# Moving four pieces of a hybrid attention layer: two matmul groups a slot later, a reduction behind a solve, and a new last block

## The chip, the cores and the metric

The kernel runs on one core of a Trainium2 chip. A core has a matrix engine (TensorE, PE in the profile, with its weight loads listed as PEld), a vector engine (VectorE, DVE), a scalar engine (ScalarE, ACT), a general engine (GpSimd, POOL), and SyncE (SP), which here issues almost all DMA transfers. Each engine works through its own queue in order. Engines wait for one another through semaphores. TensorE writes to PSUM; the other data lie in SBUF, and DRAM is reached by DMA. The metric is the device time of one execution in microseconds (us).

## The reference

The layer takes a residual stream of 256 positions by 4096 columns. One projection feeds 16 heads of forgetting attention ("fox", width 128), 32 heads of an RWKV-7 recurrence (width 64) and a gate. The gated heads go through an output projection, and a post-LayerNorm closes the layer. Cut to what matters here:

```python
proj = jnp.einsum('bsd,dc->bsc', x, w_in)
# rwkv columns: shift by one position, then split
w_raw = -jax.nn.softplus(-(w0 + jnp.tanh(wd) @ w_up)) - 0.5     # LoRA product
decay = jnp.exp(-jnp.exp(w_raw))
a = jax.nn.sigmoid(a0 + ad @ a_up)                              # LoRA product
# one step of the recurrence
sa = jnp.einsum('bhvk,bhk->bhv', state, a_t)
state = (state * w_t[:, :, None, :] + sa[..., None] * b_t[:, :, None, :]
         + v_t[..., None] * k_t[:, :, None, :])
y_t = jnp.einsum('bhvk,bhk->bhv', state, r_t)
# readout: GroupNorm of y per head, a bonus term, then
h = jnp.concatenate([fox_out, rwkv_out], axis=-1) * jax.nn.silu(z)
out = jnp.einsum('bsc,cd->bsd', h, w_out)
x = _layernorm(ALPHA * x + out, ln_gain, ln_bias, LN_EPS)
```

## The kernel before

**The main stream.** The 256 positions are two halves of 128 (`m`). Columns of the input projection come in blocks of 512. For each of eight head pairs `n` there are four blocks `b`: r and k of two 128-column groups (b = 0), v and the fox v (b = 1), and fox q, k and both gates of one group each (b = 2, 3). A block needs 32 contraction tiles. Each fp32 weight tile of two contraction tiles is split into a high and a low part: ScalarE casts the high part (L141), VectorE subtracts to get the low part (L142). Three matmuls (L147, L148, L149) then stand for one exact product, so a block is 192 main matmuls. Weights are loaded by SP three tiles ahead.

**Slots.** All other work of the layer is written as Python generators (`ahead`, `chain`, `unload`, `fox`). After every six main matmuls, `slot()` advances each generator to its next `yield`. A `yield` thus means "traced one slot later". `wait(n)` yields n times. The instructions of a slot are put behind the latest low-part split on VectorE. A planner then fixes each engine's order: it keeps the traced order where it thinks an instruction ready in time, and may move others. Two ways to bind it are used: `tc.keep_in_program_order` puts an instruction behind the one traced before it on its engine, and `tc.issue_after(i)` puts what is traced in its block behind instruction `i` on that engine. Both bind the order of issue only.

**The recurrence.** `ahead` runs `prepare(i)` for each of the 16 column groups in turn. It starts with `front(i)`: split of the LoRA weights (`uph` on ScalarE at L420, `upl` on VectorE at L422), load of the next LoRA weights (`load_up`), a `yield`, the LoRA product `lp` (L428 to L430), two Tanh, another `yield`, the decays, another `yield`. It then waits until the r and k columns of its group are there (`rk`, made at L276). The even group of a pair starts only when the pair before is `done`.

`chain` runs `rwkv(n)` for each pair. It forms the products `gp` (L534); solves a triangular system of 32 rows by 31 steps of a product and a reduce on VectorE (L601, L604), a step per slot; sends the result through DRAM (`td`, `T`); sums the values for their mean (`vm`, L616) and writes centred values into SV by eight VectorE operations (L623); builds the inverse from the blocks (`qt`, `xp`); and then goes through four chunks. A chunk has `rh` (L647), whose result R is copied by both VectorE and ScalarE (L650); `up` (L678), whose result is copied into UV (L681) by both; and, save in the last chunk, the state update `sp` (L687), from UV to the next SV (L691, L693). The readout `yp` (L707, L709) follows, then GroupNorm and the gating with the split of h (`gate`, L378, L382), and `done`. The end of block b = 2 needs `n in turned`, which `rwkv(n)` sets after `gp`.

**The output projection and the end.** Eight output blocks `b` of 512 columns follow, each with 32 contraction tiles, three matmuls each (L880 to L882), for both halves. The slots go on through most of the first two. `add(m, b)` adds the residual and takes `bn_stats`; `gain(m, b)` multiplies by the LayerNorm gain. For half 0, `moments(0)` comes while half 1's last matmuls still run. For half 1 it comes at the very end: `add(1, 7)`, the aggregation of all eight blocks' statistics (L1001), standard deviation, its reciprocal `rs`, and `s2` = mean times `rs`. A small matrix of these factors is transposed by TensorE (`zp`, `zpa`, copied as `l1` and `la`), so that one matmul with `rows` gives the LayerNorm's remaining terms for a block. Blocks 4 to 7 of half 1 (HALVED = 4) are finished by `finish`: a matmul `wp` and one VectorE operation (L1033). Blocks 0 to 3 have been gathered in PSUM with their gain; they take one matmul with `la` (L1063) and a ScalarE multiplication (L1064). Each finished block is stored by SP (L1027) in the order in which the loop writes them.

Of the kernel before, what the change touches and what calls it, by code (L numbers as in the profile page):

```python
# [10 lines left out]
F32 = mybir.dt.float32  # L11
# [6 lines left out]
P = 128  # L18
# [66 lines left out]
def layer(ctx: ExitStack, tc: tile.TileContext, xt, xtok, w_main, w_lora, w_first, muv, w_o, up, par, mulora, fbias, lng, lnb, cst, out):  # L85
# [331 lines left out]
    def front(i):  # L417
# [5 lines left out]
        load_up(i + 1)  # L423
        yield
        lp = pst(f"lp{i}")
# [94 lines left out]
    def rwkv(n):  # L520
# [78 lines left out]
        for t, s in enumerate(range(B - 2, -1, -1)):  # L599
            w = B - 1 - s  # L600
            first = nc.vector.tensor_tensor(prod[:, :, :, s + 1 :], nb[:, :, s : s + 1, s + 1 :].to_broadcast([P, 2, NJ, w]), xc[:, :, :, s + 1 :], ALU.mult)  # L601
            if not t or not n:
                tc.keep_in_program_order(first)
            nc.vector.tensor_reduce(xc[:, :, :, s : s + 1], prod[:, :, :, s:], AX.X, ALU.add)  # L604
            next(other, None)
            if t % ROWS == ROWS - 1:
                yield
# [7 lines left out]
        vt = vs_[n].rearrange("p m (u j v) -> p m u j v", u=2, j=2)  # L615
        tc.keep_in_program_order(nc.vector.tensor_reduce(vm.rearrange("p m u j -> p (m u j)"), vs_[n].rearrange("p m (a v) -> p (m a) v", v=HD), AX.X, ALU.add))  # L616
        yield
# [53 lines left out]
        for c in range(NCH):  # L671
# [11 lines left out]
            if c == NCH - 1:  # L683
                break
            sp = pst(f"sp{n}_{c}")
            for u in range(2):
# [198 lines left out]
    late = []  # L885
    st = [const.tile([P, NB, 6], F32, name=f"lst{m}") for m in range(2)]

    def add(m, b):
        acc = oacc[b]
        o = slice(b * OB, (b + 1) * OB)  # L890
        nc.vector.scalar_tensor_tensor(res[m][:, o], res[m][:, o], ALPHA, acc[m], ALU.mult, ALU.add)
        nc.vector.bn_stats(st[m][:, b, :], res[m][:, o])

# [47 lines left out]
    for b, q in outs:  # L941
# [22 lines left out]
        if b == 0:  # L964
            while sides:
                slot()
            mid.close()
            rpool = ctx.enter_context(tc.tile_pool(name="rpool", bufs=1))
            res = [rpool.tile([P, D], F32, tag=f"res{m}", name=f"res{m}") for m in range(2)]
            rows = rpool.tile([P, D], F32R, name="rows")  # L970
            nc.gpsimd.memset(rows.bitcast(F32), 0.0)
            identr = rpool.tile([P, P], F32R, name="identr")
            nc.vector.tensor_copy(identr, ident)
            for n in range(2):
                load_tok(n)
            lneps = const.tile([P, 1], F32, name="lneps")
            nc.vector.memset(lneps, LN_EPS)
# [5 lines left out]

    rss = []

    def factors(m, name):
# [4 lines left out]
    def moments(m):  # L991
# [8 lines left out]
        add(m, NB - 1)  # L1000
        nc.vector.bn_aggr(mv, st[m].rearrange("p b s -> p (b s)"))  # L1001
        mean = mv[:, 0:1]
# [4 lines left out]
        nc.vector.tensor_copy(z[:, 0:3:2], zh.bitcast(F32).to_broadcast([P, 2]))  # L1007
        last = nc.vector.tensor_tensor(z[:, 1:2], s2, zh.bitcast(F32), ALU.subtract)
        if m:
            for n, (v, at) in enumerate(((mean, (slice(0, 3, 2), slice(1, 2))), (sd, (slice(3, 5), slice(5, 6))))):  # L1010
# [44 lines left out]
    with tc.issue_after(last):  # L1055
        l1 = row(z1, "1", pp, "pp")
        la = row(za, "a", pp, "pp")
        gain(1, NB - 1)
    for n in range(HALVED):
        b = HALVED + n  # L1060
        finish(1, b, l1, pp, "pp")
        o = slice(n * OB, (n + 1) * OB)
        nc.tensor.matmul(wps[n], la, rows[:, o], start=False, stop=True)  # L1063
        nc.scalar.mul(res[1][:, o], wps[n], rss[1])  # L1064
        store(1, b, 1)
        store(1, n, 1)
# [51 lines left out]
```

## Time and profile before

| what | us |
| --- | --- |
| median of three runs | 1921.87 (1921.42 to 1925.38) |
| profiled execution | 1921.7 |
| its span, first to last instruction | 1919.5 |
| TensorE busy | 1906.1 |
| VectorE busy | 1375.6 |
| ScalarE busy | 987.3 |
| GpSimd busy | 259.1 |

A row of the timeline gives start, duration, engine, line, operation, tiles written and read, shapes, and a count where equal neighbours are merged; in brackets stands the idle time ahead of it and what ended it. Matmuls overlap one another, so the spacing of their starts says more than their durations. A row of the table of waits gives who waited for whom, the total in us, how often, and the longest. The summary of a line lists how long its engine sat idle before it and until what.

### The profile page before, as it was taken

Reading aid. Unit: us, or ns where it says so; the run is one execution under the profiler, and the core shown is the slowest. Engines: PE = TensorE matmul, PEld = TensorE weight load, DVE = VectorE, ACT = ScalarE, POOL = GpSimd, SP = SyncE. Lnnn points to the kernel's source line nnn. Section 1 sums busy time; section 2 is a strip of 40 time slices with the busy share of each in tenths; the row PEclk is TensorE's granted clock in tenths of the full one; section 3 lists DMA queues with packets and bytes.
Section 4 is the critical chain, followed back from the end, with each engine's and each line's share of the span. In section 5 each row is a group of like instructions: output and inputs, shape, how many; then the busy total and the mean of one; then the engine's idle time right before and its main releaser. Section 6 shows DMA issues by size and latency. Waiting matters only on the chain.

```text
span 1919.5 us, 27983 instructions
## 1 busy us (share of the span) xinstructions
PE 1906.1 (99%) x9785; PEld 1583.1 (82%) x9785; DVE 1375.6 (72%) x2355; ACT 987.3 (51%) x1543; POOL 259.1 (13%) x463
## 2 busy tenths in 40 slices
PE   9999999999999999999999999999999999999998
PEld 9878788888888888888888888888888878888886
DVE  7677768776876688677867786778677856755555
ACT  6554555456545644564456454645474554434333
POOL 0022012111310131013101300140013001000000
PEclk9999999999999999999999999999999999999999
DMA  9577667867686768677766776677667876766564
GB/s 344 154 232 230 193 188 229 242 202 208 209 249 194 225 204 244 195 217 217 237 199 213 223 232 203 212 225 223 206 211 221 276 257 231 253 200 202 186 203 165
DMA packets 269393, 420.04 MB, mean 219 GB/s; under 512 B 142338, under 2 KB 169364, under 8 KB 269252
## 3 DMA queue, kind: packets, MB, share of 16 engines
q1 hardware_dynamic: 268820, 417.58, 70.2%
q8 instruction: 76, 1.25, 0.3%
q10 hardware_dynamic: 432, 0.69, 0.1%
q14 instruction: 65, 0.53, 0.1%
HBM read 388.55 MB, written 29.64 MB: 218 GB/s over the span
## 4 chain that ended last, share of the span: by engine, by line
PE 96%; DVE 2%; DMA 1%; ACT 1%; issue 0%; SPq 0%; DVEq 0%; ACTq 0%
PE acc L147 24%; PE acc L149 23%; PE acc L148 23%; PE oacc L882 6%; PE oacc L880 6%; PE oacc L881 6%; PE gp L534 1%; PE rh L647 1%; PE up L678 1%; PE sp L687 1%; PE accl L149 1%; PE accl L147 1%; DMA w<-in_w_main_dram 1%; PE accl L148 0%; PE yp L709 0%
## 5 line engine op out<-in xcount | busy, mean ns | idle before, releaser
L759 POOL COPY pT<-lg 32x96 f32<-32x96 f32 x128 | 59.6, 466 | 406.7 <-DVE lg L755 402.0
L571 POOL COPY BKt<-BK 32x192 f32<-32x192 f32 x128 | 76.8, 600 | 55.2 <-DVE BK L568 50.2
L604 DVE TENSOR_REDUCE xc<-prod 128x8 f32<-128x16 f32 (+30 forms) x248 | 72.2, 291 | 5.5
L601 DVE TENSOR_TENSOR prod<-Nb,xc 128x8 f32<-128x8 f32 (+30 forms) x248 | 72.1, 291 | 3.6
L142 DVE TENSOR_TENSOR w_6l<-w,w_6h 128x1024 fp32r<-128x1024 f32 x31 | 39.8, 1283 | 40.6 <-ACT w_6h L141 23.4
L142 DVE TENSOR_TENSOR w_14l<-w,w_14h 128x1024 fp32r<-128x1024 f32 x31 | 38.0, 1225 | 39.4 <-ACT w_14h L141 33.3
L141 ACT CAST w_13h<-w 128x1024 fp32r<-128x1024 f32 x31 | 32.6, 1052 | 45.8 <-issue 12.3
L141 ACT CAST w_12h<-w 128x1024 fp32r<-128x1024 f32 x31 | 32.6, 1051 | 45.8 <-PE acc L148 26.5
L142 DVE TENSOR_TENSOR w_8l<-w,w_8h 128x1024 fp32r<-128x1024 f32 x31 | 37.8, 1220 | 25.4 <-ACT w_8h L141 17.2
L142 DVE TENSOR_TENSOR w_13l<-w,w_13h 128x1024 fp32r<-128x1024 f32 x31 | 38.3, 1234 | 23.6 <-ACT w_13h L141 12.1
L142 DVE TENSOR_TENSOR w_7l<-w,w_7h 128x1024 fp32r<-128x1024 f32 x31 | 37.9, 1222 | 20.5 <-ACT w_7h L141 8.0
L142 DVE TENSOR_TENSOR w_12l<-w,w_12h 128x1024 fp32r<-128x1024 f32 x31 | 38.9, 1256 | 18.8 <-ACT w_12h L141 10.3
L142 DVE TENSOR_TENSOR w_5l<-w,w_5h 128x1024 fp32r<-128x1024 f32 x31 | 39.7, 1282 | 16.8 <-PE acc L149 10.5
L142 DVE TENSOR_TENSOR w_11l<-w,w_11h 128x1024 fp32r<-128x1024 f32 x31 | 38.2, 1232 | 18.0 <-issue 12.4
L141 ACT CAST w_9h<-w 128x1024 fp32r<-128x1024 f32 x31 | 32.5, 1050 | 35.9 <-PE acc L148 25.5
L142 DVE TENSOR_TENSOR w_3l<-w,w_3h 128x1024 fp32r<-128x1024 f32 x31 | 37.9, 1222 | 18.0 <-ACT w_3h L141 10.2
L147 PE MATMUL acc<-w_5h,x 128*128 128x512 f32 x124 | 50.6, 408 | 0.0
L147 PE MATMUL acc<-w_8h,x 128*128 128x512 f32 x124 | 50.5, 408 | 0.0
L149 PE MATMUL acc<-w_2l,x 128*128 128x512 f32 x124 | 48.4, 391 | 1.4 <-DVE w_2l L142 1.4
L147 PE MATMUL acc<-w_15h,x 128*128 128x512 f32 x124 | 49.6, 400 | 0.0
L147 PE MATMUL acc<-w_11h,x 128*128 128x512 f32 x124 | 49.1, 396 | 0.4 <-ACT w_11h L141 0.4
L147 PE MATMUL acc<-w_9h,x 128*128 128x512 f32 x124 | 49.5, 399 | 0.0
(812 smaller groups left out, 6605.1 us busy)
## 6 DMA issues: line engine op xcount, KB each, us to landing
w<-in_w_main_dram SPq DMA_DIRECT2D x496, 512.0 KB
wo<-in_w_o_dram SPq DMA_DIRECT2D x128, 512.0 KB
bt<-bk SPq DMA_DIRECT2D x88, 128.0 KB
Nb<-nd SPq DMA_DIRECT2D x16, 512.0 KB
hd<-hl SPq DMA_DIRECT2D x29, 256.0 KB
h<-hd SPq DMA_DIRECT2D x29, 256.0 KB
wr<-in_w_first_dram SPq DMA_DIRECT2D x15, 384.0 KB
lr<-in_w_lora_dram SPq DMA_DIRECT2D x14, 336.0 KB
```

The costliest lines, as they stand in the source:

```text
L141: nc.scalar.copy(hi[:, :n], src[:, :n])
L142: latest[0] = nc.vector.tensor_tensor(lo[:, :n], src[:, :n], hi[:, :n].bitcast(F32), ALU.subtract)
L147: nc.tensor.matmul(acc[:, :n], xs[k][:, 0, tt], hi[:, o : o + n], start=(k == 0), stop=False)
L148: nc.tensor.matmul(acc[:, :n], xs[k][:, 1, tt], hi[:, o : o + n], start=False, stop=False)
L149: nc.tensor.matmul(acc[:, :n], xs[k][:, 0, tt], lo[:, o : o + n], start=False, stop=(k == KT - 1))
L571: nc.gpsimd.tensor_copy(BKt[B * b : B * (b + 1), :, :, B * a : B * (a + 1)], BK[B * a : B * (a + 1), :, : NCH - 1, B * b : B * (b + 1)])
L601: first = nc.vector.tensor_tensor(prod[:, :, :, s + 1 :], nb[:, :, s : s + 1, s + 1 :].to_broadcast([P, 2, NJ, w]), xc[:, :, :, s + 1 :], ...
L604: nc.vector.tensor_reduce(xc[:, :, :, s : s + 1], prod[:, :, :, s:], AX.X, ALU.add)
L759: (nc.gpsimd.tensor_copy if b % 2 else nc.scalar.copy)(pT[B * b : B * (b + 1), :, B * a : B * (a + 1)], lg[B * a : B * (a + 1), :, B * b : ...
L880: nc.tensor.matmul(acc, ht[k][:, 0, tt], hi, start=(k == 0), stop=False)
L881: nc.tensor.matmul(acc, ht[k][:, 1, tt], hi, start=False, stop=False)
L882: nc.tensor.matmul(acc, ht[k][:, 0, tt], lo, start=False, stop=(k == KT - 1))
```

## The change

- `front`: the LoRA product is traced two slots after the split of its weights, not one.
- `rwkv`: one more `yield` stands ahead of the update `sp` of each chunk but the last.
- `rwkv`: the reduce that makes `vm` is queued behind the last reduce of the solve on VectorE, and no longer behind whatever was traced there just before.
- The end: for half 1, the statistics of output blocks 0 to 6 are aggregated when block 6 is done, and kept as one triple (count, mean, count times variance) beside the six numbers of block 7, so that the last aggregation reads 9 columns and not 48.
- The end: block 4 of half 1 is finished by VectorE alone. Its gain and bias are loaded early into `own`, broadcast over the partitions. Two operations then give `res * rs - (gain * s2 - bias)`, and it is stored first. `gain(1, 7)` comes later, just ahead of the finish of block 7.

```diff
@@ front
         load_up(i + 1)
-        yield
+        yield from wait(2)
         lp = pst(f"lp{i}")
@@ rwkv
-            nc.vector.tensor_reduce(xc[:, :, :, s : s + 1], prod[:, :, :, s:], AX.X, ALU.add)
+            solved = nc.vector.tensor_reduce(xc[:, :, :, s : s + 1], prod[:, :, :, s:], AX.X, ALU.add)
...
-        tc.keep_in_program_order(nc.vector.tensor_reduce(vm.rearrange("p m u j -> p (m u j)"), vs_[n].rearrange("p m (a v) -> p (m a) v", v=HD), AX.X, ALU.add))
+        with tc.issue_after(solved.ins):
+            nc.vector.tensor_reduce(vm.rearrange("p m u j -> p (m u j)"), vs_[n].rearrange("p m (a v) -> p (m a) v", v=HD), AX.X, ALU.add)
...
             if c == NCH - 1:
                 break
+            yield
             sp = pst(f"sp{n}_{c}")
@@ add
+    sums = const.tile([P, 9], F32, name="sums")
...
-        nc.vector.bn_stats(st[m][:, b, :], res[m][:, o])
+        nc.vector.bn_stats(sums[:, 3:] if m and b == NB - 1 else st[m][:, b, :], res[m][:, o])
+        if m and b == NB - 2:
+            nc.vector.bn_aggr(sums[:, 1:3], st[m][:, : NB - 1].rearrange("p b s -> p (b s)"))
+            nc.vector.memset(sums[:, 0:1], float(b * OB + OB))
+            nc.vector.tensor_scalar(sums[:, 2:3], sums[:, 2:3], float(b * OB + OB), None, ALU.mult)
@@ after output block 0
+            own = rpool.tile([P, 2, OB], F32, name="own")
+            for j, src in enumerate((lng, lnb)):
+                nc.sync.dma_start(out=own[:, j, :], in_=src[:, HALVED * OB : (HALVED + 1) * OB].to_broadcast([P, OB]))
@@ moments
-        nc.vector.bn_aggr(mv, st[m].rearrange("p b s -> p (b s)"))
+        nc.vector.bn_aggr(mv, sums if m else st[m].rearrange("p b s -> p (b s)"))
...
+        s2s.append(s2)
@@ the end, half 1
     with tc.issue_after(last):
         l1 = row(z1, "1", pp, "pp")
         la = row(za, "a", pp, "pp")
-        gain(1, NB - 1)
+        o = slice(HALVED * OB, (HALVED + 1) * OB)
+        nc.vector.scalar_tensor_tensor(own[:, 0, :], own[:, 0, :], s2s[1], own[:, 1, :], ALU.mult, ALU.subtract)
+        ahead_ = nc.vector.scalar_tensor_tensor(res[1][:, o], res[1][:, o], rss[1], own[:, 0, :], ALU.mult, ALU.subtract)
+        store(1, HALVED, 1)
     for n in range(HALVED):
         b = HALVED + n
-        finish(1, b, l1, pp, "pp")
+        with tc.issue_after(ahead_.ins):
+            if b == NB - 1:
+                gain(1, b)
+            if n:
+                finish(1, b, l1, pp, "pp")
         o = slice(n * OB, (n + 1) * OB)
         nc.tensor.matmul(wps[n], la, rows[:, o], start=False, stop=True)
         nc.scalar.mul(res[1][:, o], wps[n], rss[1])
-        store(1, b, 1)
+        if n:
+            store(1, b, 1)
         store(1, n, 1)
```

1 line of the change is left out of this document (added).

## The prediction

> **What bounds the kernel now.** I read the page first, then the table of who waited for whom on TensorE, then single places in the timeline.
>
> ```profile
> span 1919.5 us, 27983 instructions
> PE 1906.1 (99%) x9785; PEld 1583.1 (82%) x9785; DVE 1375.6 (72%) x2355; ACT 987.3 (51%) x1543; POOL 259.1 (13%) x463
> ```
>
> TensorE (PE) is busy in all but 13.4 us of the span. The change removes one matmul of 9785, so it can save time in three places only: stalls between matmuls, the end, where TensorE has run dry, and the start, which it does not touch. The table of waits names the stalls long enough to be counted one by one:
>
> ```profile
> PE acc L149 <- DVE w_2l L142: 1.4, 1, 1.4
> PE zp L1020 <- DVE zd L1008: 1.4, 1, 1.4
> ...
> PE acc L149 <- DVE w_10l L142: 1.0, 1, 1.0
> PE up L678 <- ACT R L650: 0.9, 1, 0.9
> PE acc L147 <- ACT w_11h L141: 0.4, 1, 0.4
> ```
>
> Each occurs once. Everything that this change can win is of this size: single microseconds in 1900. A change of 0.2% (3.8 us of the median of 1921.87) is about what a measurement of this kernel can tell from none.
>
> The sum below is made against the profiled execution: 1921.7 us, of which 1919.5 are span and 2.2 lie around it. The median of the runs is 0.2 us above it, so I count the two as one.
>
> **Part 1: the state update a slot later.** For three of the four chunks of a pair, the matmul `sp` (L687) is now traced one slot, six main matmuls, after `up`. It reads UV, which ScalarE and VectorE copy out of PSUM (L681). The summary of line 687, and three of its groups in the timeline, each with the main matmul before and after:
>
> ```profile
>   DVE UV L681: 3.5, 13
> ```
>
> ```profile
> 615.04 0.39 PE L149 MATMUL acc<-w_6l,x 128*128 128x512 f32 x1
> ...
> 615.64 0.48 PE L147 MATMUL acc<-w_7h,x 128*128 128x512 f32 x1
> ...
> 606.72 0.40 PE L149 MATMUL acc<-w_4l,x 128*128 128x512 f32 x1
> ...
> 607.39 0.47 PE L147 MATMUL acc<-w_4h,x 128*128 128x512 f32 x1
> ...
> 623.25 0.40 PE L149 MATMUL acc<-w_9l,x 128*128 128x512 f32 x1
> ...
> 623.98 0.48 PE L147 MATMUL acc<-w_9h,x 128*128 128x512 f32 x1
> ```
>
> From start to start the first group takes 0.60 us, the second 0.67, the third 0.73: the last two lose 0.07 and 0.13 us. The summary counts 13 such waits; its 3.5 us adds idle time of the weight-load queue to that of the array, so it is no price. Thirteen times 0.07 to 0.13 is 0.9 to 1.7 us. I take 1.4, since the larger loss is the more frequent. It should go wholly: one slot is six times the 0.23 us between main matmuls, 1.4 us, and no wait here is longer than a tenth of that. From below I allow nothing gained. The yield adds no instruction, DMA or semaphore.
>
> What becomes later is the chain behind it: the three updates move the readout of a pair and `done` by three slots, and with Part 2 by four, 5.5 us. The next to wait for that is `prepare` of the next pair, which starts with the LoRA product. In the rows below its first matmul is at 842.45 and VectorE first touches the new r and k columns at 857.63, 15.2 us later.
>
> ```profile
> 842.45 0.28 PE L428 MATMUL lp<-lr,uph 96*128 96x256 f32 x1
> ...
> 843.85 0.34 PE L430 MATMUL lp<-lr,upl 96*128 96x256 f32 x1
> 844.03 0.28 PE L428 MATMUL lp<-lr,uph 96*128 96x256 f32 x1
> ```
>
> ```profile
> 857.63 0.88 DVE L276 SCALAR_TENSOR_TENSOR s<-raw,prm,s 128x255 f32<-128x255 f32 x2
> ```
>
> Two more slots of `front` follow the product (2.8 us), so 12.4 us are spare, against 5 slots needed (6.9 us). The pair loop therefore does not grow, and I cost the delay at nothing. If that cover were gone, `chain` would slip by the missing slots in each pair, until `turned` held back the next eviction.
>
> **Part 2: the LoRA product a slot later.** L430 reads `upl`, which VectorE makes at L422. The summary of line 430 and a clean group:
>
> ```profile
>   DVE upl L422: 1.3, 6
> ```
>
> ```profile
> 871.01 0.28 PE L430 MATMUL lp<-lr,upl 96*128 96x256 f32 x1
> 871.13 0.28 PE L428 MATMUL lp<-lr,uph 96*128 96x256 f32 x1
> ```
>
> A clean L430 is followed after 0.12 us. The one at 843.85 took 0.18, so it lost 0.06. Six such waits give 0.4 us from below and the summary gives 1.3 from above (again with the load queue's idle time). I take 0.6, near the lower end, because that end is a spacing of the array itself. The extra slot lies ahead of the two Tanh on ScalarE (L432, L434) and all of `front` behind them, whose cover is the 12.4 us just counted. `load_up` keeps its place on SP.
>
> **Part 3: the sum of the values behind the solve.** The wait of 1.4 us for w_2l stands in the first pair. The VectorE rows ahead of it, and the matmul that waited:
>
> ```profile
> 208.17 0.68 DVE L616 TENSOR_REDUCE vm<-vs 128x8 f32<-128x512 f32 x1
> ...
> 209.17 0.28 DVE L623 SCALAR_TENSOR_TENSOR SV<-vm,vs 64x128 f32<-64x128 f32 x1
> ...
> 214.66 1.22 DVE L142 TENSOR_TENSOR w_2l<-w,w_2h 128x1024 fp32r<-128x1024 f32 x1
> ...
> 217.25 0.41 DVE L604 TENSOR_REDUCE xc<-prod 128x8 f32<-128x256 f32 x1
> ```
>
> ```profile
> 215.93 0.50 PE L149 MATMUL acc<-w_2l,x 128*128 128x512 f32 x1 [1.45 <-DVE w_2l L142]
> ```
>
> VectorE has no gap in this stretch. The reduce (0.68) and eight STT of 0.28 stand between the last steps of the solve and ahead of the split: 2.9 us that nothing needs before `rh`. Behind the last step of the solve, they also stand behind w_2l, which starts ahead of the last step now (its reduce is the row at 217.25). 2.9 us is more than 1.45, so I take the whole 1.4. The ends are 1.4 gained and, if the same 2.9 us then delay a later split by as much, nothing. In the later pairs the same move wins nothing, because the table has no wait there.
>
> **Part 4: the end.** The rows of the tail, from the aggregation to the stores, and the stretch in which the stores run:
>
> ```profile
> 1908.14 0.37 DVE L1001 BATCH_NORM_AGGREGATE mv<-lst 128x2 f32<-128x48 f32 x1
> ...
> 1909.08 0.16 DVE L1005 TENSOR_TENSOR s<-mv,rs 128x1 f32<-128x1 f32 x1
> ...
> 1909.67 0.68 DVE L896 TENSOR_TENSOR res<-res,lg 128x512 f32<-128x512 f32 x1
> ...
> 1910.40 0.27 ACT L1022 CAST la<-zpa 128x128 fp32r<-128x128 f32 x1
> ...
> 1911.09 2.81 DVE L1033 SCALAR_TENSOR_TENSOR res<-res,rs,wp 128x512 f32<-128x512 f32 x4 [0.74 <-PE wp L1032]
> ...
> 1911.33 2.09 ACT L1064 ACTIVATE res<-wp,rs 128x512 f32<-128x512 f32 x3 [0.65 <-PE wp L1063]
> ```
>
> ```profile
> 1911.87 0.81 SPq L1027 DMA_DIRECT2D out_dram<-res  x2
> ```
>
> ```profile
> 1913.00:1918.00 5.00, 0.54 (x2) 0.00 (x0) 0.90 (x2) 1.10 (x2) 0.00 (x0) 0.50 1.03 382
> ```
>
> The last eight stores are 2.1 MB, and at 382 GB/s with a DMA share of 1.03 they need 5.5 us, 0.69 each. The DMA engines are the bound from the first of these stores on, so the end moves with the first, as long as the next ones are there. The aggregation shrinks from 48 elements to 9: between the 0.37 of today and the 0.16 of a one-column operation I take 0.27, a gain of 0.1. Then `own` takes two STT, each priced at the 0.70 of L1033 (2.81 for four), from 1909.57: done at 1910.97, so that the first store leaves at about 1911.0 and not at 1911.87, 0.9 us sooner. The second is ScalarE's first product, ready at about 1911.9 (1911.33 less 0.1, and 2.09 / 3 = 0.70). It follows the first by 0.9 us, and the first keeps the engines for 0.69, which leaves a hole of 0.2. Gain 0.6 to 0.7, of which I take 0.6; the ends are 0 (stores bound by their data) and 0.9. VectorE's total from 1909.57 on is two STT, the gain and three finishes, 4.2 us, so its last block is ready at 1913.8, when only four stores have gone: covered. One matmul fewer shortens nothing by itself.
>
> TensorE's clock shows here too: the stretch above was granted 0.50, after the 1.4 us that the table of waits shows ahead of `zp`. [...]
>
> The other additions: two broadcast loads of 256 KB into `own` on SP after output block 0, at most 0.52 MB at 382 GB/s, 1.4 us of transfer ahead of the next weight loads. I cost them at nothing, since the table of waits has no TensorE wait for a DMA; uncovered, they cost 1.4 us. The early aggregation, memset and scale after block 6 are 0.7 us of VectorE beside projection matmuls, and nothing is queued behind them but `gain` and the splits of block 7.
>
> **The sum.** 1.4 + 0.6 + 1.4 + 0.6 = 4.0 us: 1921.7 - 4.0 = 1917.7. The waits for w_10l, R and w_11h are outside the edits; I count them as unchanged.
>
> **Rivals.** *The written slot is not the issued place.* At 842.45 and 843.85 the two matmuls L428 and L430 are written back to back and issued 1.4 us apart, with main matmuls between: the order is made by a planner with its own idea of what is ready. If it puts `sp` and L430 again right behind their producers, Parts 1 and 2 win nothing: 1921.7 - 2.0 = 1919.7. Against it: the 13 waits of line 687 come about because `sp` stands where it is written, close behind its producers.
>
> *The re-timed chain makes new single waits.* For it speak the four waits of the table, all at places where VectorE, ScalarE or the SP queue bunch up, and one of the long SP waits, from the table of the SP queue between 265 and 300 us:
>
> ```profile
> SPq L281 <- DVE tw L436: 5.4, 1, 5.4
> ```
>
> In the first two pairs the chain moves most. Four new waits like the four listed are 3.7 us, and the time would be 1921.4. Against it: the wait for w_11h follows that SP wait, and a later `front` takes the LoRA operations out of its way, so it may as well win 0.4.
>
> *Slower: the readout meets the block boundary.* The split with little lead in the steady pairs is w_2l, just after output of block 0 of a pair:
>
> ```profile
> 836.81 0.42 DVE L378 SCALAR_TENSOR_TENSOR h<-post,zr 128x256 f32<-128x256 f32 x1
> ...
> 838.73 1.22 DVE L142 TENSOR_TENSOR w_2l<-w,w_2h 128x1024 fp32r<-128x1024 f32 x1
> ```
>
> ```profile
> 841.55 0.39 PE L149 MATMUL acc<-w_2l,x 128*128 128x512 f32 x1
> ```
>
> It is ready at 839.95, 1.6 us ahead of its use. The readout of a pair is two halves of four operations like the one of 0.42, 3.4 us. If four slots' delay put all of it newly ahead of one such split, TensorE would wait 1.8 us in each of six pairs, 10.8 us: 1921.7 - 4.0 + 10.8 = 1928.5. It decides from 2.9 us of extra VectorE work ahead of the split (1.6, and 7.8 us over six pairs). Against it: half of that work stands ahead of this split already, and moving it later takes it away from there.
>
> **How the numbers follow.** Forecast 0.50, with a range of its own from 1916.0 (the waits for R and w_11h go as well) to 1919.0 (Part 3 or Part 4 falls short). Planner's order 0.13, new waits 0.21, slower 0.11, and 0.05 that more waits go than I count, below 1916. Faster by over 0.2% is below 1918.0: four fifths of the forecast and the last case, 0.45 less a little for noise, 0.44. Slower is above 1925.7: 0.11 and a little of the new waits, 0.13. Within: 0.43. The range from 1915.8 to 1922.5 holds all cases but the slower one and the far end.
>
> **What would show it.** Part 1: no idle time on line 687. Part 2: none on L430. Part 3: L616 and L623 behind the last L604 in every pair, and no wait for w_2l. Part 4: the first of the last eight stores leaves SP some 0.9 us sooner relative to the aggregation, and the end follows by 0.6. The prediction is wrong if the table of TensorE's waits has new rows over 1 us, or if pairs come further apart than they do now.

## The result and the profile after

The changed kernel takes 1917.48 us (median of 14 runs, 1916.41 to 1920.35), the kernel before 1922.75 (median of 14, 1921.42 to 1925.61): a ratio of 0.9975, with a 95% interval from 0.9968 to 0.9982. That is a gain of some 5 us, where 1917.7 was predicted. The profiled execution of the changed kernel took 1917.13 us, with a span of 1915.3, 4.2 us below that of before.

Line numbers behind the edits move by two or more: the update `sp` is L689 now, its result UV is copied at L682, `vm` is at L617 and SV at L624. First the head of the page, which has the busy time, its share of the span and the instructions of each engine:

```profile
span 1915.3 us, 27998 instructions
PE 1903.0 (99%) x9784; PEld 1584.8 (83%) x9784; DVE 1398.3 (73%) x2359; ACT 985.9 (51%) x1543; POOL 261.5 (14%) x463
```

TensorE idles for 12.3 us of the span now, against 13.4. So most of the gain is not idle time in the sense of this line: its busy time fell by 3.1 us with one matmul fewer. A main matmul lasts 0.39 us and the next one starts 0.23 after it, so one that starts up to 0.16 us late leaves no idle time behind; the spacing of the starts shows it. The table of who waited for whom on TensorE, complete down to 0.2 us:

```profile
PE warmup L108 <- POOL idle L105: 1.3, 1, 1.3
PE zp L1032 <- DVE zd L1019: 1.3, 1, 1.3
PE acc L149 <- DVE w_10l L142: 1.0, 1, 1.0
PE accl L147 <- ACT wl0h L141: 0.7, 1, 0.7
PE acc L149 <- DVE w_9l L142: 0.4, 1, 0.4
PE sp L689 <- DVE UV L682: 0.3, 1, 0.3
PE wp L1044 <- ACT l L1034: 0.2, 1, 0.2
PE ctp L357 <- DVE frest L351: 0.2, 1, 0.2
```

The waits for w_2l (1.4), R (0.9) and w_11h (0.4) are gone. The prediction had counted on the first alone. Two rows are new: `sp` for UV, 0.3 us, in the last pair, where the group starts 0.5 us late, and w_9l, 0.4 us at 99 us, a row that every other changed kernel of this study also has, at 0.2 to 0.4.

The update and LoRA groups in the timeline of TensorE, with the main matmul before or after:

```profile
617.83 0.39 PE L149 MATMUL acc<-w_9l,x 128*128 128x512 f32 x1
618.05 0.60 PE L689 MATMUL sp<-UV,BKt 128*128 128x128 f32 x4
618.41 0.48 PE L147 MATMUL acc<-w_9h,x 128*128 128x512 f32 x1
...
857.93 0.28 PE L429 MATMUL lp<-lr,uph 96*128 96x256 f32 x1
858.05 0.28 PE L430 MATMUL lp<-lr,upl 96*128 96x256 f32 x1
858.16 0.28 PE L428 MATMUL lp<-lr,uph 96*128 96x256 f32 x1
858.28 0.28 PE L429 MATMUL lp<-lr,uph 96*128 96x256 f32 x1
858.40 0.28 PE L430 MATMUL lp<-lr,upl 96*128 96x256 f32 x1
858.52 0.39 PE L147 MATMUL acc<-w_9h,x 128*128 128x512 f32 x1
```

From the main matmul ahead to the one behind, an update group takes 0.58 us now (617.83 to 618.41), where two groups of before took 0.67 and 0.73. The LoRA matmuls follow each other every 0.12 us, and L430 loses nothing.

The first pair's solve on VectorE, and the matmul that had waited 1.45 us for w_2l (six of the eight operations that write SV fall into this view):

```profile
210.34 1.22 DVE L142 TENSOR_TENSOR w_2l<-w,w_2h 128x1024 fp32r<-128x1024 f32 x1
...
217.49 0.42 DVE L604 TENSOR_REDUCE xc<-prod 128x8 f32<-128x256 f32 x1
217.82 0.68 DVE L617 TENSOR_REDUCE vm<-vs 128x8 f32<-128x512 f32 x1
218.53 1.51 DVE L624 SCALAR_TENSOR_TENSOR SV<-vm,vs 64x128 f32<-64x128 f32 x6
```

```profile
215.71 0.39 PE L149 MATMUL acc<-w_2l,x 128*128 128x512 f32 x1
```

`vm` stands behind the last reduce of the solve, and w_2l is ready at 211.56, 4.1 us ahead of its use. In all eight pairs `vm` starts 0.33 to 0.34 us after the start of that reduce.

The tail, on VectorE, SP and TensorE, and three stretches of it (busy time of each engine, granted clock, DMA share, GB/s):

```profile
1904.47 0.20 DVE L1012 BATCH_NORM_AGGREGATE mv<-sums 128x2 f32<-128x9 f32 x1
...
1905.82 0.75 DVE L1071 SCALAR_TENSOR_TENSOR own<-own,s 128x512 f32<-128x512 f32 x1
...
1906.60 0.75 DVE L1072 SCALAR_TENSOR_TENSOR res<-res,rs,own 128x512 f32<-128x512 f32 x1
```

```profile
1907.39 0.33 SPq L1039 DMA_DIRECT2D out_dram<-res  x1
...
1908.19 0.33 SPq L1039 DMA_DIRECT2D out_dram<-res  x1
```

```profile
1907.40:1908.20 0.80, 0.80 (x5) 0.63 (x4) 0.80 (x2) 0.73 (x2) 0.00 (x0) 1.00 0.00 0
1908.20:1909.00 0.80, 0.41 (x2) 0.00 (x0) 0.80 (x2) 0.80 (x2) 0.00 (x0) 1.00 0.86 328
1909.00:1913.00 4.00, 0.00 (x0) 0.00 (x0) 1.03 (x2) 0.90 (x2) 0.00 (x0) 0.84 1.00 378
```

The first of the last eight stores leaves 2.92 us after the aggregation begins, against 3.73. The second follows 0.80 us later, and in the stretch behind it the DMA engines reach a share of 0.86 only.

**Where the 4.2 us lie.** The starts of the main matmuls cut both spans into stages (a pair is 768 main matmuls, an output block 192):

| stage | before | after | difference |
| --- | --- | --- | --- |
| start to the first block of the second pair | 208.43 | 209.81 | +1.38 |
| from there to the last block of the second pair | 148.70 | 145.12 | -3.58 |
| six pair periods from there | 1140.10 | 1138.15 | -1.95 |
| end of the pairs and output blocks 0 to 3 | 233.07 | 233.55 | +0.48 |
| output blocks 4 to 7, to the last statistics | 177.11 | 177.11 | 0.00 |
| last statistics to the end | 12.12 | 11.60 | -0.52 |

The rows sum to -4.19. The first is scatter for the most part: in all kernels of this study the first main matmul of these blocks comes at 5.5 to 6.6 us and the second block 62.3 to 64.5 later, whichever edits were in, and two kernels below that differ only behind the pairs (without the update edit, and the kernel from these parts) have 208.40 and 209.70 in this row. The +0.48 is mostly output block 2, 43.86 against 43.52. The largest gain is in one stretch of 149 us, in which the first pair's recurrence runs.

### The profile page after: what moved, and what is told of

Its sections match the earlier page's. It is cut to its first block, busy times and chain, and to the rows that moved or that the text cites. A ratio compares the mean times of both kernels' runs of the same rounds, so it can differ in the third digit from the quotient of the medians.

```text
span 1915.3 us, 27998 instructions
## 1 busy us (share of the span) xinstructions
PE 1903.0 (99%) x9784; PEld 1584.8 (83%) x9784; DVE 1398.3 (73%) x2359; ACT 985.9 (51%) x1543; POOL 261.5 (14%) x463
## 4 chain that ended last, share of the span: by engine, by line
PE 97%; DVE 1%; ACT 0%; issue 0%; DMA 0%; DVEq 0%; ACTq 0%
PE acc L147 24%; PE acc L149 24%; PE acc L148 24%; PE oacc L884 6%; PE oacc L882 6%; PE oacc L883 6%; PE rh L648 1%; PE gp L534 1%; PE up L679 1%; PE sp L689 1%; PE accl L147 1%; PE accl L148 1%; PE accl L149 1%; PE yp L711 0%; PE yp L709 0%; PE fsp L746 0%
## 5 line engine op out<-in xcount | busy, mean ns | idle before, releaser
L142 DVE TENSOR_TENSOR w_0l<-w,w_0h 128x1024 fp32r<-128x1024 f32 x31 | 38.7, 1248 | 38.2 <-ACT w_0h L141 25.0
L142 DVE TENSOR_TENSOR w_9l<-w,w_9h 128x1024 fp32r<-128x1024 f32 x31 | 38.0, 1225 | 21.6 <-issue 8.0
L142 DVE TENSOR_TENSOR w_10l<-w,w_10h 128x1024 fp32r<-128x1024 f32 x31 | 38.0, 1224 | 20.6 <-ACT w_10h L141 8.0
L142 DVE TENSOR_TENSOR w_15l<-w,w_15h 128x1024 fp32r<-128x1024 f32 x31 | 38.0, 1226 | 19.4 <-issue 15.9
L141 ACT CAST w_8h<-w 128x1024 fp32r<-128x1024 f32 x31 | 32.6, 1052 | 37.6 <-DMA w<-in_w_main_dram 12.5
L141 ACT CAST w_1h<-w 128x1024 fp32r<-128x1024 f32 x31 | 32.7, 1054 | 34.8 <-DMA w<-in_w_main_dram 18.9
L147 PE MATMUL acc<-w_14h,x 128*128 128x512 f32 x124 | 49.5, 399 | 0.0
L147 PE MATMUL acc<-w_1h,x 128*128 128x512 f32 x124 | 49.1, 396 | 0.0
L147 PE MATMUL acc<-w_2h,x 128*128 128x512 f32 x124 | 49.1, 396 | 0.0
L147 PE MATMUL acc<-w_0h,x 128*128 128x512 f32 x124 | 49.1, 396 | 0.0
```

The costliest lines, as they stand in the source:

```text
L141: nc.scalar.copy(hi[:, :n], src[:, :n])
L142: latest[0] = nc.vector.tensor_tensor(lo[:, :n], src[:, :n], hi[:, :n].bitcast(F32), ALU.subtract)
L147: nc.tensor.matmul(acc[:, :n], xs[k][:, 0, tt], hi[:, o : o + n], start=(k == 0), stop=False)
```

## The experiments

Two accounts were tried against each other. By the prediction's, the change is a sum of independent terms, each removed from TensorE at its own place, and the delay of the chain is hidden. By its rival, the delay decides: it moves the recurrence against the main stream, so that the waits that go are those which happen to stand in the way, and the loop from one pair to the next grows. An expectation that names theories by letters uses the letters for that run alone.

To see the delay, I count in each trace the slot at which `gp` of a pair is issued: a slot is six main matmuls, a pair has 128, and slot 0 is the pair's first main matmul.

| kernel | slot of `gp`, first pair, second, ... |
| --- | --- |
| before | 82, 77, 74, 74, ... |
| update edit alone | 82, 80, 78, 76, 74, 74 |
| LoRA edit alone | 83, 80, 77, 75, 75, ... |
| LoRA edit in the first pair alone | 83, 78, 74, 74, ... |
| after without the update edit | 83, 80, 77, 75, ... |
| after | 83 in every pair |
| after, update one slot later again | 83, 86, 89, 92, 95, 96, 96, 96 |

**The sum of the values alone.** The kernel before, with (`solved` is the reduce of the solve, as in the diff of the change)

```diff
-        tc.keep_in_program_order(nc.vector.tensor_reduce(vm..., vs_[n]..., AX.X, ALU.add))
+        with tc.issue_after(solved.ins):
+            nc.vector.tensor_reduce(vm..., vs_[n]..., AX.X, ALU.add)
```

> The kernel before with the reduce of the values behind the solve, and nothing else of the change. Theory A (each part takes away its own wait): the wait of 1.4 us for w_2l in the first pair is gone, those for w_11h (0.4), R (0.9) and the 13 of the update stay, and the time is 1.4 us shorter. Theory B (the later chain re-times the first two pairs, and that is what took the waits away): the wait for w_2l stays at over 0.5 us, and the time is within 0.5 us of the kernel before.

Measured: 1922.51 us, ratio 0.9999 (0.9989 to 1.0008). The wait for w_2l is gone, and the table of waits of this kernel has a new row:

```profile
PE qt L639 <- DMA T<-td: 0.7, 1, 0.7
```

`qt` needs the solved system back from DRAM. With the 1.6 us stall removed TensorE arrives there sooner, at about 223 us, and the round trip is not done. By the starts of the main matmuls, the eight slots around `qt` take 1.5 us more than before, and the stretch of the first pair's recurrence shrinks from 148.70 to 148.37 only. So Part 3 does what the prediction says, and it is worth nothing by itself, because the next thing that is late stands 8 us behind.

**The update alone.** The kernel before, with

```diff
             if c == NCH - 1:
                 break
+            yield
             sp = pst(f"sp{n}_{c}")
```

> The kernel before with the update a slot later, and nothing else. Theory A: the waits of the update fall from 13 to 2 or fewer, w_2l keeps its 1.4, w_11h its 0.4; 1.4 us shorter. Theory B: the readout of the first pair comes 3 slots later, front of the second pair is no longer in the way of the shifts, and the wait for w_11h goes too, as does that for R in the last pair: 2.5 to 3 us shorter, and 8 blocks of a pair repeat at 189.8 us in the steady state in place of 190.0.

Measured: 1924.14 us, ratio 1.0008 (0.9998 to 1.0017): no gain, if anything a loss. The waits of the update for UV fall from 13 to 2. I worked out from the starts of all matmuls in one steady pair (the sixth to the seventh) what each group costs: from the main matmul ahead to the one behind, the three update groups take 1.76 us a pair and not 1.99, a gain of 0.23, but the groups around the LoRA product lose 0.32 more, and the pair comes 190.13 after the one before, against 190.01. The larger loss lies in the first three of the six pair periods (191.88, 190.50 and 191.12 us), where `gp` is still falling back; the second pair's recurrence has a new wait of 1.2 us for w_1l there. What puts the LoRA product at a worse place is not shown; that it moves is, since it comes after the readout of the pair before, which is three slots later.

**The LoRA product alone.** The kernel before, with

```diff
         load_up(i + 1)
-        yield
+        yield from wait(2)
```

> The kernel before with the LoRA product a slot later, and nothing else. Theory A: no idle time on L430, 0.6 us shorter, w_2l, w_11h and R as before. Theory B: w_11h changes by more than 0.3 us in either direction, and the start (the waits for w_9l and w_10l) gets up to 0.5 us longer, since front of the first group moves beside the first shifts; within 0.5 us of the kernel before.

Measured: 1919.66 us, ratio 0.9987 (0.9978 to 0.9996). This edit, priced at 0.6, carries more than half of the whole gain. The stretch of the first pair's recurrence takes 145.55 us against 148.70, and the waits for w_2l and w_11h are gone, although `vm` is bound as before. In the second pair's recurrence stands a new wait for w_1l of 1.2 us, and line 430, which was to wait no more, has one wait of 0.8 us left.

**The LoRA product in the first pair alone.** To see whether this comes from line 430 or from the shift:

```diff
         load_up(i + 1)
-        yield
+        yield from wait(2 if i < 2 else 1)
```

> The kernel before, with the LoRA product a slot later in the first pair alone (its two column groups); the later pairs keep one slot. Theory A (what the LoRA edit buys is the shift of the first pair by a slot, which takes the waits of pairs 0 and 1 away; the waits of line 430 are worth little): pairs 0 and 1 take about 145.6 us from the first block of the second pair to its last, and not 148.7, as with the LoRA edit everywhere; the readiness of the products gp sits at slot 83 in the first pair and then falls back as before; time 1919.5 to 1920.5, ratio about 0.9986. Theory B (the gain comes from the waits of line 430 in all pairs): at most a third of it, 0.2 us from line 430 itself and 148.7 us for the stretch, time about 1922.5, ratio 0.9999. If the stretch is short and a new wait of 1 to 1.5 us for a low part stands in the second pair, as with the LoRA edit alone, theory A holds with its price.

Measured: 1919.02 us, ratio 0.9981 (0.9972 to 0.9991), no less of a gain than with the edit in all pairs. The stretch takes 145.69. In the later pairs everything is as before: they come 190.0 apart, and line 430 has its six waits, 1.6 us in the summary. So the LoRA edit pays by moving the recurrence of the first pair by a slot. VectorE in that pair, of this kernel, shows how:

```profile
208.30 1.22 DVE L142 TENSOR_TENSOR w_2l<-w,w_2h 128x1024 fp32r<-128x1024 f32 x1
...
215.45 0.42 DVE L604 TENSOR_REDUCE xc<-prod 128x8 f32<-128x256 f32 x1
215.78 0.68 DVE L616 TENSOR_REDUCE vm<-vs 128x8 f32<-128x512 f32 x1
216.49 2.02 DVE L623 SCALAR_TENSOR_TENSOR SV<-vm,vs 64x128 f32<-64x128 f32 x8
```

Here `vm` still has its old binding, behind whatever is traced just before it, and it stands behind the solve all the same: a slot later, that is where the order puts it. The LoRA edit thus does Part 3's work in the one place where the kernel before gives Part 3 any, and since `qt` is a slot later too (slot 12 of the next pair, not 11), the round trip through DRAM is done in time.

**The changed kernel without the new binding of the sum.**

```diff
-        with tc.issue_after(solved.ins):
-            nc.vector.tensor_reduce(vm..., vs_[n]..., AX.X, ALU.add)
+        tc.keep_in_program_order(nc.vector.tensor_reduce(vm..., vs_[n]..., AX.X, ALU.add))
```

> The changed kernel with the reduce of the values bound as before. Theory A (parts add up): the one wait for w_2l in the first pair comes back, 1.4 us, about 1918.9. Loop theory (update and LoRA edits together make the loop of a pair exactly as long as a pair's 128 slots, so that every pair keeps the late phase of the first): the reduce and the writes of SV stand ahead of a split at the same late place in every pair, and a wait of about 1.4 us comes in each of seven or eight pairs: pairs 191 us apart in place of 189.7, about 1927, slower than the kernel before.

Measured: 1917.80 us, ratio to before 0.9973 (0.9961 to 0.9984), the same as the changed kernel. No wait for w_2l comes back, in no pair. Both accounts had expected a loss, and both were wrong. The two traces show why: from the first instruction to the last matmul, TensorE, VectorE, GpSimd and SP run through the same order of instructions in both kernels, and so does ScalarE up to its last products. With both shifts in, the new binding asks for what the order has anyway.

Beside one shift alone it does not. In the two runs with a single shift and the old binding (the update alone, the LoRA product alone), the second pair's eight writes of SV stand ahead of w_1l, and that is the wait of 1.2 us; in the runs with the same shift and the new binding (the next two), they stand behind the solve, and the wait is gone. VectorE with the LoRA edit alone, and with the new binding beside it (the run without the update edit, below):

```profile
401.22 0.29 DVE L623 SCALAR_TENSOR_TENSOR SV<-vm,vs 64x128 f32<-64x128 f32 x1
...
401.87 1.22 DVE L142 TENSOR_TENSOR w_1l<-w,w_1h 128x1024 fp32r<-128x1024 f32 x1
```

```profile
396.84 1.22 DVE L142 TENSOR_TENSOR w_1l<-w,w_1h 128x1024 fp32r<-128x1024 f32 x1
...
402.05 0.68 DVE L617 TENSOR_REDUCE vm<-vs 128x8 f32<-128x512 f32 x1
```

The pairs of runs also differ in the edits of the end, whose tail is worth 0.5 us. Their medians fall by 2.6 us (1919.66 to 1917.11) beside the LoRA edit and by 4.1 (1924.14 to 1920.09) beside the update edit.

**The changed kernel without the LoRA edit.**

```diff
-        yield from wait(2)
+        yield
         lp = pst(f"lp{i}")
```

> The changed kernel with the LoRA product at its old slot. Theory A: 0.6 us back, about 1918.1. Loop theory: the loop is 126 slots, gp goes from 82 back to 74 by two slots a pair as it did with the update alone, L430 waits 0.27 us in several pairs again, and pairs come 190.1 apart: 1.5 to 3 us slower than the changed kernel, about 1920.5.

Measured: 1920.09 us, ratio 0.9983 (0.9973 to 0.9993), 2.6 us above the changed kernel. The stretch of the first pair takes 147.03, with the wait of `qt` for T in it (0.6), steady pairs come 190.1 apart, and output block 2 has lost 1.8 us.

**The changed kernel without the update edit.**

```diff
             if c == NCH - 1:
                 break
-            yield
             sp = pst(f"sp{n}_{c}")
```

> The changed kernel with the update at its old slot. Theory A: 1.4 us back, about 1918.9, with 13 waits of the update. Loop theory: the loop is 125 slots, gp goes from 83 back to 75 as with the LoRA edit alone, there the update did not wait in the steady pairs, so there are fewer than 5 waits of the update, pairs 189.8 apart, and the time is within 1 us of the changed kernel.

Measured: 1917.11 us, ratio 0.9968 (0.9956 to 0.998): as fast as the changed kernel. Its steady pairs come 189.77 apart, against 189.67 with the update edit, so that edit is worth 0.1 us a pair here and not 0.23: with the LoRA shift alone the update's waits for UV have fallen to 7 already. One pair has a wait of 1.0 us on line 430 and comes 191.09 after the one before. In the traces the six periods take 1.8 us more than with the update edit (1139.95 and 1138.15), but the start takes 1.4 less, and the medians do not tell the two kernels apart.

**One slot more for the update.** The changed kernel, with

```diff
                 break
-            yield
+            yield from wait(2)
             sp = pst(f"sp{n}_{c}")
```

> The changed kernel with the update two slots later in place of one. Theory A (12.4 us of cover): another three slots are hidden; within 0.5 us of the changed kernel. Loop theory: the loop of a pair is 131 slots against 128, so gp moves three slots later in each pair (83, 86, 89, 92, 95 of 128) until the end of block 2 holds it at 96; from then on slots are spent without matmuls, and the pairs come 190.5 to 194 us apart: 3 to 12 us slower than the changed kernel.

Measured: 1929.96 us, ratio 1.0036 (1.0024 to 1.0048), 12.5 us above the changed kernel. The table of slots says why. In the kernel before, `gp` falls back by five slots from the first pair to the second, so the loop from a pair to the next takes 123 slots of the 128. The LoRA edit adds two (its drift is -3), the update three (its drift is -2). With both the loop takes 128, exactly a pair: the changed kernel keeps the late phase of the first pair and stays there. Three slots more, and each pair slips by three, until `gp` sits at slot 96, where the block of b = 2 cannot end before `turned`. From the third of the six periods on they take 190.7 to 192.3 us. The longest is the third, before `gp` has come to 96, and TensorE shows no wait at the end of a block; the waits that it shows stand where the late chain now falls (w_14l at slot 28 of the next pair, R at slot 30). So the slip and its end at 96 are shown, and a price of the hold at `turned` itself is not. The table of waits of TensorE of this kernel:

```profile
PE fop L766 <- POOL pT L761: 3.1, 1, 3.1
PE oacc L884 <- DVE wo_4l L142: 1.4, 1, 1.4
PE oacc L882 <- ACT hl L381: 1.4, 1, 1.4
...
PE acc L149 <- DVE w_14l L142: 0.9, 2, 0.5
```

The six periods account for 6.7 us of the loss, and most of the rest lies where the end of the chain meets output blocks 0 to 2, with the first three rows.

**The end alone.** The kernel before, with the edits in `add`, `moments`, after output block 0 and in the last loop, as in the diff above.

> The kernel before with the two edits of the end, and nothing else. Theory A: from the transpose of half 1's factors to the end of the span 0.3 to 0.4 us less than before, and 0.1 to 0.2 less ahead of it: 0.5 us shorter; all waits of the pairs as before. Theory B agrees here. If the two loads into own or the early aggregation cost something, a wait over 0.2 us appears in output blocks 1 to 7.

Measured: 1922.83 us, ratio 0.9998 (0.9989 to 1.0007). The tail from the last statistics to the end takes 11.61 us against 12.12, a gain of 0.51, where the changed kernel has 0.52. But the profiled execution loses 1.8 us in the stretch of the first pair (w_11h: 1.6 us here, 0.4 before; `qt` for T: 0.5 here), where the order of instructions is the same as before, and 0.92 in output block 2. A gain of 0.5 us is below what the median tells from none.

**The end with its loads later.** To see whether the loads into `own` cost those 0.92 us:

```diff
             own = rpool.tile([P, 2, OB], F32, name="own")
-            for j, src in enumerate((lng, lnb)):
-                nc.sync.dma_start(out=own[:, j, :], in_=src[:, ...].to_broadcast([P, OB]))
...
+        if b == 4:
+            for j, src in enumerate((lng, lnb)):
+                nc.sync.dma_start(out=own[:, j, :], in_=src[:, ...].to_broadcast([P, OB]))
```

> The kernel before with both edits of the end, as in the run of the end alone, but with the two loads into own issued after output block 4 and not after output block 0. Theory A (the loads disturb the projection where they are issued: the stage from the last block of the pairs' weights to the one after took 44.44 us there and 43.52 before): that stage falls back to 43.52, no stage behind output block 4 grows by more than 0.1, and the whole gains the tail's 0.5 us against before: time about 1922.2, ratio 0.9997, and about 0.6 below the run of the end alone. Theory B (the loads cost nothing; the 0.92 us there is the planner's other order of VectorE work near the end of the chain): the stage stays at 44.4, and the time at 1922.8. The median alone may not tell them apart; the stage does.

Measured: 1922.40 us, ratio 0.9998 (0.9988 to 1.0007). Output block 2 takes 43.52 again, and no later block grew. That speaks for the loads, but it does not separate them from the order: with the loads moved, VectorE also has some of the low-part splits of these output blocks in another order. And the changed kernel without the new binding of the sum has the loads at the early place and also took 43.52 there, where the changed kernel, with the same order, took 43.86; kernels without any such loads took 43.69 (the LoRA edit in the first pair) and 44.01 (the update alone). What the loads cost stays open.

**The statistics whole.** The changed kernel without the early aggregation:

```diff
-        nc.vector.bn_stats(sums[:, 3:] if m and b == NB - 1 else st[m][:, b, :], res[m][:, o])
-        if m and b == NB - 2:
-            ...
+        nc.vector.bn_stats(st[m][:, b, :], res[m][:, o])
...
-        nc.vector.bn_aggr(mv, sums if m else st[m].rearrange("p b s -> p (b s)"))
+        nc.vector.bn_aggr(mv, st[m].rearrange("p b s -> p (b s)"))
```

> The changed kernel with the statistics of half 1 aggregated whole at the end (48 columns), and everything else kept. Separates the two edits of the end. From the aggregation to the last product zp: 1.90 us (1.72 in the changed kernel), that is 0.18 later for the first store and for the end, so the tail from the last statistics to the end takes about 11.8 us (11.6 changed, 12.1 before); the rest of the tail's gain is the block finished by VectorE. If the aggregation's length does not set the end (another engine ends it), the tail stays at 11.6.

Measured, from one profiled execution: from the aggregation to `zp` 1.90 us (1.72 in the changed kernel), and from the last statistics to the end 11.77 (11.60). So the shorter aggregation is worth 0.17 of the 0.52, and the block finished by VectorE 0.35.

This run shows something else. It took 1920.45 us, and 148.20 in the stretch of the first pair, not 145.12, although the order of instructions on all five engines is the same as in the changed kernel up to the output projection, but for one memset of one column that VectorE does at the very start. By the starts of the main matmuls, the 3.1 us lie in two places. 1.3 lie at 234 us, where `up` waited 1.1 us for R. The other 1.8 lie at 324 us, and ScalarE's rows ahead of that place, in this kernel and in the changed one, show where they come from:

```profile
313.91 0.41 ACT L420 CAST uph<-upt 96x256 fp32r<-96x256 f32 x1 [2.62 <-DMA upt<-in_up_dram]
```

```profile
311.76 0.41 ACT L420 CAST uph<-upt 96x256 fp32r<-96x256 f32 x1 [0.19 <-DMA upt<-in_up_dram]
```

SP issued this load at 308.65 and at 308.57. By the casts that waited for it (started at 313.91 and at 311.76), it landed 2.15 us later in the one execution than in the other. Behind the cast on ScalarE stand the exponentials of the decays that VectorE needs, and behind VectorE's work on those stands w_5l, for which TensorE then waited 1.5 us. Two more stages differ without an edit in them: the start took 1.5 us less than in the changed kernel, and output blocks 0 and 1 had a wait of 2.0 us for wo_7h.

**A kernel from these parts.** The changed kernel without the update edit, and with the loads into `own` after output block 4:

```diff
-            yield
             sp = pst(f"sp{n}_{c}")
...
-            for j, src in enumerate((lng, lnb)):
-                nc.sync.dma_start(out=own[:, j, :], ...)
...
+        if b == 4:
+            for j, src in enumerate((lng, lnb)):
+                nc.sync.dma_start(out=own[:, j, :], ...)
```

> The changed kernel without the update edit, and with the two loads into own issued after output block 4: the version that the runs so far point to. If the update edit is worth nothing beside the others and the loads cost what the stage showed: 1916.5 to 1917.3, ratio about 0.9968, at or below the changed kernel's 1917.5. If the update edit is worth its 1.4 us as predicted: 1918.5 to 1919.

Measured: 1917.25 us, ratio 0.9971 (0.996 to 0.9983). Not slower than the changed kernel, and not to be told from it. No kernel of this study beats it by what the medians can show.

## Why the prediction was right, and where its steps were not

The total, 1917.7 against 1917.48, came out of a sum whose terms were partly misplaced.

**The sum as such.** Alone, the sum edit changes the median by nothing (-0.2 us), the update edit by +1.4 (its interval reaches -0.4), the LoRA edit by -3.1 and the end by nothing (+0.1): -1.9 in all, where the whole change gives -5.3. So "1.4 + 0.6 + 1.4 + 0.6" is not how the gain is made. It comes near for the profiled pair of traces, but not for the parts one by one, and that the total was met to 0.2 us is in part luck: terms that were not foreseen, on both sides, made up for each other.

**Part 1.** "I take 1.4 ... It should go wholly." In the changed kernel it nearly did: in a steady pair the update groups fell from 1.99 to 1.77 us, and over the six pair periods these groups gain 1.2. The waits of line 689 are two now, in the first pair and in the last. The step that failed is the next: "12.4 us are spare, against 5 slots needed (6.9 us). The pair loop therefore does not grow, and I cost the delay at nothing." The loop grew, from 123 slots to 128, exactly a pair. That it fits is what saves the gain: the 5 slots were all the spare there was, and three more cost 12.5 us. I had counted the time from the LoRA product to the first use of the r and k columns, which is a stretch of one pair. The spare of a loop is read from the drift from pair to pair (82, 77, 74), which the trace of before shows. And alone this part wins nothing: the LoRA groups lose what the update groups gain, and w_1l of the second pair is late. With Parts 3 and 4 beside it and the LoRA edit left out, the kernel is 2.7 us faster than before.

**Part 2.** "I take 0.6." In the six pair periods the groups of the LoRA product gain 0.6 in all (0.3 of it in the first): the term is right. But the edit's worth is another: by moving the first pair by a slot it takes 3 us from one stretch, as the run with the edit in the first pair alone shows.

**Part 3.** "I take the whole 1.4." The wait went, and `vm` and SV are behind the solve in every pair. By itself that gave way to the wait of `qt` for its DMA, 0.7 us, and the median did not move: the lower end of the range ("delay a later split by as much, nothing") was the right one, by another wait. In the changed kernel Part 2 alone would have removed the wait. "In the later pairs the same move wins nothing" holds for the kernel before, but the shifts of Parts 1 and 2, taken singly, make a new place for it, w_1l in the second pair.

**Part 4.** "Gain 0.6 to 0.7, of which I take 0.6": 0.52 was measured. The sum was right in kind and 0.1 too large. The first store is 0.81 us sooner relative to the aggregation (0.9 predicted); the aggregation took 0.20 and not 0.27; the two operations into `own` took 0.75 each and not 0.70; the hole behind the first store is 0.29 (7.66 us from the first store to the end before, 7.95 after) and not 0.2, because the second store came 0.80 us after the first. The memset that I had put beside output block 6 is done at the start of the kernel. The early loads, "at nothing", are open by up to 0.9.

**"The waits for w_10l, R and w_11h ... I count them as unchanged."** w_10l stayed at 1.0. R and w_11h went, 1.3 us by the table, and the wait of `sp` in the last pair is new. The record tells which edit did it: R in the last pair is gone in every kernel with the update edit and stays, at 0.6 to 0.9, in every kernel without it; w_11h is gone in every kernel with the update or the LoRA edit and stays, at 0.2 to 1.7, in those with neither. This is the part of the gain that the prediction left to its range.

**The clock.** The prediction says of the tail of before that "the stretch above was granted 0.50"; the sum has no term for it. In the changed kernel the drop came behind the last product, which starts at 1908.21: the stretches above show 1.00 until 1909.00 and 0.84 from there to 1913.00, and the last products follow each other every 0.23 to 0.24 us. So no product was slowed here.

**The rivals.** The planner did not undo the shifts of Parts 1 and 2, but its order, not the binding, decided the place of `vm` in the run with the LoRA edit in the first pair. New single waits are what the parts alone ran into (w_1l 1.2, T 0.7, line 430 up to 1.2). The slower case was wrong in its place, w_2l after a block boundary; a slower one of its size was one yield per chunk away. There the chain slipped by the missing slots in each pair up to slot 96, as the prediction had said of a cover that is gone, but the time was lost along the late chain and where its end meets the output blocks.

## What to carry to other kernels

In a loop in which a side chain feeds its own next round, count the loop in the units of the main stream, and read its spare from the drift of a marker from round to round: here 5 slots of 128, of which the change used all. A wait that occurs once, where two orders of work happen to meet, is cheap to remove by shifting one of them, but what is next late stands close behind, so that such edits do not add; try them one by one and all but one. An edit that does nothing alone and nothing as the last one in can still pay in between, as the binding of the sum does beside either shift. And a difference of some 3 us in one stage of a single trace may be two late events and no edit at all: see how far that stage scatters between kernels of the same order before crediting the edit.

## What the runs showed of the hardware

- Two executions with the same order of instructions in a stretch of the main loop differed by 3.1 us in it (148.20 and 145.12), 1.3 where R was late and 1.8 behind the load into `upt`, which was issued within 0.1 us of the same time and used 2.15 us later in the one. A third with that order took 145.87. Of the eight kernels with the LoRA edit, the other seven took 145.1 to 145.9 there, and the six without it 147.0 to 150.9, so here the stage agrees with the medians; one trace by itself could have misled.
- The clock granted to TensorE fell in both tails, in the one among the last products and in the other behind them. Before, 1908 to 1912 us was granted 0.94 and 1912 to 1918 0.50; the last three products follow 0.42 to 0.43 us apart, where the two at 1911.13 and 1911.36 had followed after 0.24 and 0.23. After, the last product starts at 1908.21; 1907.4 to 1909.0 was granted 1.00 and 1909 to 1913 0.84. By the trace of before the slower products did not set the end: VectorE and ScalarE were done with their last blocks at 1913.91 and 1914.27, and from 1913 to 1918 the stores kept the DMA engines at a share of 1.03.
- An aggregation of 9 columns took 0.20 us and one of 48 columns 0.37. If the time grows evenly between these two, that is an estimate of 0.0044 us a column over some 0.16.
